# A 2 KB bias row fetched one unit ahead, and the first feed-forward weights used on the ready token blocks first

## The chip, the cores and the metric

One Trainium2 chip, 8 NeuronCores in two dies (cores 0 to 3, 4 to 7). The same program runs on all 8 cores, with no exchange between them. The metric is the device time of the slowest core in microseconds.

Engine names in profile lines: PE is TensorE (PEld its weight loads), DVE is VectorE, ACT is ScalarE, POOL is GpSimd, SP is SyncE; SPq marks the issue of a transfer by SP. In this kernel POOL issues the loads that cast from float32 to bf16 (all large weights), SP all other loads and all stores.

## The reference, cut to what matters

One layer of a diffusion backbone. Each core handles 12 tiles of 128 tokens (4 of context, 8 of latents). The order of the work on a core:

```
mod  = silu(c) @ w_ada + b_ada                 # six chunks of 2048; chunks 2 and 5 are the gates g1, g2
h    = modulate(rms_norm(x), sh1, sc1)
att  = differential_attention(h);  sgu = spatial_gating(h)
x1   = x + g1 * (concat(att, sgu) @ w_o)       # "projection"
h2   = modulate(rms_norm(x1), sh2, sc2)
y    = x1 + g2 * (relu(h2 @ w_ff1)**2 @ w_ff2) # "feed-forward", half of the time
```

The modulation matmuls are cut into 32 units. They run as filler between attention matmuls; units 16 to 31 make the gates, and each needs a row of 256 bias values for two conditions: 2 KB.

## The kernel before

The kernel has its own scheduler. It keeps an estimated clock for each engine and emits each instruction where that clock says TensorE would otherwise wait. So a change to one load changes the estimates, and with them the order of attention. In the traces every core runs the instructions of an engine in one and the same order, so an instruction that waits holds up those behind it. Cuts are marked `# ...`.

A gate unit. The bias row is loaded in the step that uses it:

```python
def ada_step():
    # ...
    ada_mm(wring[2], bank, 256)                  # 16 small matmuls
    mod_r.take()
    if chunk >= 2:
        S.load(brw, brow[chunk - 2, :, u * 256:(u + 1) * 256], "brw")
    nd = S.copy(modl, bank[:, 0:256])
    if i + 1 < 32:
        ada_dma1(i + 1)                          # 1 MB of weights for the next unit
    def fin(bj):
        # ...
            S.mm([(b2[0:2, 0:256], sel_t, modl, True, True)], 450)
            nd = S.tt(gst, b2[0:2, 0:256], brw, ALU.add)      # VectorE waits here for the bias
```

What is emitted after attention. POOL's queue runs ahead of TensorE, so these are issued as soon as their space is free:

```python
    for gi in range(4):
        wu_dma(gi)                               # gating "up" weights, 4 loads
    wo_dma(1)                                    # output projection, 1 of 4 blocks
    S.load(wsb, wsT, "wsb", cast=True)
    S.load(flat(bs_t), bsb, "bsb")
    S.load(sgw, sgunw, "sgw")                    # norm weights of the gating
```

The passage from the projection to the feed-forward. `norm2` normalises a finished token tile, and a delayed part `tr` transposes it on TensorE and, after every fourth tile, modulates 512 tokens on VectorE:

```python
    xm_r = Lot(S, [S.sbuf("xm%d" % i, [128, D], BF16, z1 + 8 * K + 4 * K * i) for i in range(2)])
    wf_r = [S.sbuf("wf%d" % i, [128, 4096], BF16, f0 + 8 * K * i) for i in range(2)]   # f0 = z1 + 8 K
    # ...
    for tt in range(12):
        wo_tile(tt)
        norm2(tt)
        wo_loads(tt + 3)
        if tt == 0:
            wf_dma()                             # first feed-forward weights
        S.pump()
    S.flush()                                    # the last tile's transposes and modulations
    wf_dma()                                     # second feed-forward weights
    # ...
    gate_load(1, g2_t)
    for tt in range(12):
        S.load(acc[:, tt, :], x1d[tt], "acc%d" % tt, dr=[("x1", tt)])     # residual
    for rd in range(8):
        for j in range(4):
            W = wf_s.pop(("1", rd, j)).rearrange("p (k n) -> p k n", k=16)
            for f in range(2):
                for tb in range(3):              # token blocks of 512
                    # 16 matmuls of 512 columns into one PSUM bank, relu (ACT), square (DVE)
            wf_dma()
        # then the four weight units of the second matrix
```

The first of the two feed-forward weight buffers lies over both `xm` buffers.

## Time and profile before

| | before |
|---|---|
| median of 3 runs | 2581.16 us |
| PE busy | 93% of the span |
| feed-forward, first to last matmul (core 2) | 1327.2 us, 6144 matmuls, 216 ns each |
| PE waits for an attention bank held up by the last bias load | 14.9 us (core 2) |
| PE waits for the last normalised tile | 5.5 us (all cores) |

The page of the slowest core (2) begins with the busy time of PE. Below it, in 40 slices of the span, stand the tenths in which PE was busy and its granted clock in tenths of full speed:

```profile
PE 2413.2 (93%) x16816; PEld 1390.6 (54%) x16816; DVE 1299.5 (50%) x2536; ACT 713.0 (28%) x1157; POOL 99.1 (4%) x164
...
PE   1469999999999979999999999999999999999999
...
PEclk9679999999999989999999999999999999999999
```

The reader sees an engine that is nearly always busy, with two visible weaknesses: the first tenth of the span, where the kernel waits for its first weights and which the change leaves alone, and one slice in the middle (the fifteenth, 904 to 968 us) with a lower digit in both rows. The last half of the rows is the feed-forward at full clock. There the change can win nothing.

**The slice in the middle.** POOL's queue at that time (columns: start, length, engine, line, operation, tiles; in brackets the idle time before it and what ended it). These weights are queued in two microseconds:

```profile
893.66 0.54 POOL L319 DMA_DIRECT2D wu_11985<-wu  x1
...
895.74 0.58 POOL L319 DMA_DIRECT2D wo_11994<-wo  x1
```

The same stretch on the other engines:

```profile
901.24 0.40 SPq L319 DMA_DIRECT2D brw<-brow  x1
...
905.91 0.59 PE L256 MATMUL ps<-modl,sel_t 128*2 128x256 f32 x2
...
909.89 1.02 ACT L272 ACTIVATE P_108<-ps 128x1024 bf16<-128x1024 f32 x1
923.20 0.41 DVE L288 TENSOR_TENSOR gst<-ps,brw 2x256 f32<-2x256 f32 x1 [17.43 <-DMA brw<-brow]
...
924.26 0.41 DVE L288 TENSOR_TENSOR o_115<-ps,st_67 128x256 f32<-128x256 f32 x1
...
924.82 1.02 PE L256 MATMUL ps<-VV_96,P_110 128*128 128x129 bf16 x8 [14.90 <-DVE o_115 L288]
```

The bias load is issued at 901.24. The unit's small matmul is done at 906.5. VectorE then sits until 923.20 for a 0.41 us addition, because the 2 KB have not landed. Behind it in VectorE's order is `o_115`, which empties an attention bank (a bank of PSUM, the memory that TensorE's results go to); TensorE has used up its other work by 909.9 us and waits for that bank. The view of waits for 895 to 925 us (total, times, longest) gives both:

```profile
DVE gst L288 <- DMA brw<-brow: 17.4, 1, 17.4
PE ps L256 <- DVE o_115 L288: 14.9, 1, 14.9
```

Two stores of attention results stand just ahead of the bias row in SP's own queue, at 899.8 and 900.8 us. The view of DMAs issued from 899.7 to 901.3 us (size, time from issue to landing) shows that they are late as well:

```profile
attd<-on_119 SPq DMA_DIRECT2D x1, 64.0 KB, 11.8
attd<-on_117 SPq DMA_DIRECT2D x1, 64.0 KB, 20.3
```

So the second store lands at 921.1 us. The single packets in the packed trace (`prof` has no view of them) say the same: the next two packets of 1 KB in that queue, which by size and order are the bias row, move only at 921.5 us. On all eight cores the store ahead of the row takes 20 to 26 us. By order and times the row waits behind slow stores in its own queue; what made that queue slow is tested below (weights_late).

**The start of the feed-forward.** The timeline from the last projection matmuls on:

```profile
1242.88 1.89 PE L256 MATMUL ps<-wo_11996,sguT 128*128 128x512 bf16 x8
...
1248.86 1.29 DVE L295 TENSOR_SCALAR xm_13138<-xw_13136,st_68 128x2048 bf16<-128x2048 f32 x1 [2.63 <-ACT st_68 L272]
...
1250.29 1.87 PE L263 MATMUL ps<-identb,xm_13138 128*128 128x128 bf16 x16 [5.52 <-DVE xm_13138 L295]
...
1251.95 4.28 PE L256 MATMUL ps<-hT,wf_13142 128*128 128x512 bf16 x13
1252.38 0.15 PEld L256 LDWEIGHTS ps<-hT,wf_13142 128*128 128x128 bf16 x1 [0.28 <-issue]
1252.40 3.97 DVE L295 TENSOR_SCALAR hT<-hT,A_47,S_48 128x512 bf16<-128x512 bf16 x12 [2.25 <-ACT hT L272]
1252.45 0.53 POOL L319 DMA_DIRECT2D wf_13141<-wf  x1 [179.37 <-PE ps L263]
1252.80 0.15 PEld L256 LDWEIGHTS ps<-hT,wf_13142 128*128 128x128 bf16 x1 [0.28 <-issue]
```

TensorE finishes the projection at about 1244.8, then waits 5.52 us while ACT and DVE normalise the last tile, and transposes it. The weight loads at 1252.38 and 1252.80 show the spacing of the first matmuls: 0.43 us and not 0.216. The modulations at 1252.40 are needed only by token block 2; blocks 0 and 1 were ready long before.

The Trainium skill, page "TensorE: Matmul & The Clock Gate", section "Part 1: The HAM clock gate", says that the array falls to half its clock after an idle window of about 3.4 us and comes back after about as long a busy one. The trace agrees: after both waits the granted clock reads 0.50, from 924.8 to 930.0 us and from 1250.0 to 1254.5 us.

### The profile page before, as it was taken

To read this page: it belongs to the slowest core of one execution; us is meant where nothing else is said; L and a number is where in the kernel's file an instruction comes from. 1 tells how busy PE (TensorE), PEld (TensorE's weight loads), DVE (VectorE), ACT (ScalarE), POOL (GpSimd) and SP (SyncE) were. 2 spreads that over 40 slices of the span, in tenths; PEclk is the share of its full clock that TensorE was granted. 3 is DMA by queue.
4 is the path that set the end of the run, shared out by engine and by line. 5 is a ranking of instruction groups with operands and counts; after the bars stand their busy time and mean duration, and the time that the engine had idled before them with its cause. 6 is when DMAs were issued, how large, how long until landed. Compare 5 with 4: busy or idle time off the path is not lost.

```text
span 2583.1 us, 39598 instructions; the slowest of 8 cores (2572.3 to 2583.1 us)
## 1 busy us (share of the span) xinstructions
PE 2413.2 (93%) x16816; PEld 1390.6 (54%) x16816; DVE 1299.5 (50%) x2536; ACT 713.0 (28%) x1157; POOL 99.1 (4%) x164
## 2 busy tenths in 40 slices
PE   1469999999999979999999999999999999999999
PEld 0358777777767765444444444444444444444444
DVE  1258563663663435455338165282562834717437
ACT  1146672773853753133210100101001010010110
POOL 0002100000000000000000000000000000000000
PEclk9679999999999989999999999999999999999999
DMA  9974543444355545744752332222222332222246
GB/s 188 189 191 129 83 89 68 85 81 80 66 92 103 97 86 87 175 166 144 186 140 50 55 57 52 49 49 50 49 49 52 57 56 49 49 49 49 50 94 184
DMA packets 58843, 237.17 MB, mean 92 GB/s; under 512 B 20336, under 2 KB 26032, under 8 KB 35376
## 3 DMA queue, kind: packets, MB, share of 16 engines
q0 software_dynamic: 22848, 150.25, 33.3%
q1 hardware_dynamic: 35824, 84.41, 10.0%
q8 instruction: 136, 2.23, 0.3%
q14 instruction: 35, 0.29, 0.0%
HBM read 352.34 MB, written 32.54 MB: 149 GB/s over the span
## 4 chain that ended last, share of the span: by engine, by line
PE 84%; DMA 8%; DVE 4%; ACT 3%; issue 0%; POOL 0%; another core or an unknown queue 0%; SPq 0%; DVEq 0%
PE ps L256 83%; DMA sel_t<-selsum 2%; DMA ada_122<-wa 2%; PE ps L263 1%; DMA xt_130<-xs 1%; DMA kr_106<-ck 1%; DMA wr_90<-wa 1%; DMA brw<-brow 1%; DMA kr_105<-ck 0%; DVE hT L295 0%; ACT P_110 L272 0%; ACT P_107 L272 0%; ACT P_109 L272 0%; DMA xt_129<-xs 0%
## 5 line engine op out<-in xcount | busy, mean ns | idle before, releaser
L256 PE MATMUL ps<-hT,wf_13142 128*128 128x512 bf16 x1536 | 335.4, 380 | 0.0
L256 PE MATMUL ps<-wf_13142,aT 128*128 128x512 bf16 x1536 | 334.1, 379 | 0.0
L256 PE MATMUL ps<-hT,wf_13141 128*128 128x512 bf16 x1536 | 334.1, 379 | 0.0
L256 PE MATMUL ps<-wf_13141,aT 128*128 128x512 bf16 x1536 | 334.1, 379 | 0.0
L272 ACT ACTIVATE rl_14431<-ps 128x512 f32<-128x512 f32 x96 | 57.3, 597 | 855.2 <-PE ps L256 855.2
L256 PEld LDWEIGHTS ps<-hT,wf_13142 128*128 128x128 bf16 x1536 | 150.4, 98 | 182.2 <-issue 1.7
L256 PEld LDWEIGHTS ps<-wf_13142,aT 128*128 128x128 bf16 x1536 | 150.5, 98 | 181.0
L256 PEld LDWEIGHTS ps<-hT,wf_13141 128*128 128x128 bf16 x1536 | 150.4, 98 | 181.1
L256 PEld LDWEIGHTS ps<-wf_13141,aT 128*128 128x128 bf16 x1536 | 150.2, 98 | 181.3
L288 DVE TENSOR_TENSOR aT<-rl_14432 128x512 bf16<-128x512 f32 x96 | 66.5, 693 | 264.9 <-ACT rl_14432 L272 264.9
L288 DVE TENSOR_TENSOR aT<-rl_14431 128x512 bf16<-128x512 f32 x96 | 66.5, 693 | 262.1 <-ACT rl_14431 L272 262.1
L288 DVE TENSOR_TENSOR tf_14433<-ps,g_t 128x512 f32<-128x512 f32 x192 | 132.8, 692 | 59.2 <-PE ps L256 59.2
L288 DVE TENSOR_TENSOR tf_14434<-ps,g_t 128x512 f32<-128x512 f32 x192 | 132.8, 692 | 58.8 <-PE ps L256 58.8
L256 PE MATMUL ps<-wr_88,hT 128*128 128x256 bf16 x1152 | 151.4, 284 | 6.9 <-DVE hT L295 4.6
L288 DVE TENSOR_TENSOR acc<-acc,tf_14434 128x512 f32<-128x512 f32 x192 | 132.9, 692 | 7.0
L288 DVE TENSOR_TENSOR acc<-acc,tf_14433 128x512 f32<-128x512 f32 x192 | 132.9, 692 | 7.0
L272 ACT ACTIVATE rl_14432<-ps 128x512 f32<-128x512 f32 x96 | 57.3, 597 | 274.2 <-PE ps L256 274.2
L256 PEld LDWEIGHTS ps<-wr_88,hT 128*128 128x128 bf16 x1152 | 111.7, 101 | 30.3 <-issue 15.5
L256 PE MATMUL ps<-wr_89,hT 128*128 128x256 bf16 x960 | 124.3, 276 | 0.7 <-ACT fz_97 L272 0.4
L272 ACT ACTIVATE P_107<-ps 128x1024 bf16<-128x1024 f32 x76 | 77.6, 1020 | 129.1 <-PE ps L256 129.1
L256 PEld LDWEIGHTS ps<-wr_89,hT 128*128 128x128 bf16 x960 | 91.0, 99 | 14.5 <-issue 4.1
L272 ACT ACTIVATE P_109<-ps 128x1024 bf16<-128x1024 f32 x76 | 77.5, 1019 | 30.8 <-PE ps L256 30.6
(802 smaller groups left out, 2827.7 us busy)
## 6 DMA issues: line engine op xcount, KB each, us to landing
wr_90<-wa POOLq DMA_DIRECT2D x32, 1024.0 KB, 9.2
wf_13142<-wf POOLq DMA_DIRECT2D x32, 1024.0 KB, 8.0
wf_13141<-wf POOLq DMA_DIRECT2D x32, 1024.0 KB, 8.0
acc<-x1d SPq DMA_DIRECT2D x12, 1024.0 KB, 42.1
ys<-acc SPq DMA_DIRECT2D x32, 256.0 KB, 2.4
ada_121<-wa POOLq DMA_DIRECT2D x3, 2048.0 KB, 26.5
ada_122<-wa POOLq DMA_DIRECT2D x3, 2048.0 KB, 38.9
wr_88<-wqkv POOLq DMA_DIRECT2D x6, 1024.0 KB, 10.1
```

What stands on the lines that cost most here:

```text
L256: ins = e.matmul(o, lhsT=l, rhs=r, start=st, stop=sp, skip_group_check=True)
L263: ins = e.transpose(o, i, ident)
L272: return self.add("act", lambda e: e.activation(out=out, in_=in_, func=func, bias=bias, scale=scale, **kw), reads=[in_] + aps, writes=[out ...
L288: return self.add(eng, lambda e: e.tensor_tensor(out=out, in0=a, in1=b, op=op), reads=[a, b], writes=[out], cost=self.dcost(eng, out, (a, b)))
```

## The change

Three intents. First, fetch the bias row one unit ahead, into a second buffer. Second, start the feed-forward with the token blocks that are ready, and put the last tile's transposes behind the first of that work; for this the second `xm` buffer moves away from under the weight buffer. Third, issue the second feed-forward weights earlier and mix the residual reloads between the weight loads.

```diff
-    brw = S.sbuf("brw", [2, 256], F32, p1 + 10 * K)
+    brw = [S.sbuf("brw%d" % i, [2, 256], F32, b) for i, b in enumerate((p1 + 10 * K, SB + 13 * K))]
@@ ada_step
-        if chunk >= 2:
-            S.load(brw, brow[chunk - 2, :, u * 256:(u + 1) * 256], "brw")
         nd = S.copy(modl, bank[:, 0:256])
         if i + 1 < 32:
+            c2, u2 = divmod(i + 1, 8)
+            if c2 >= 2:
+                S.load(brw[(i + 1) % 2], brow[c2 - 2, :, u2 * 256:(u2 + 1) * 256], "brw%d" % ((i + 1) % 2))
             ada_dma1(i + 1)
-                nd = S.tt(gst, b2[0:2, 0:256], brw, ALU.add)
+                nd = S.tt(gst, b2[0:2, 0:256], brw[i % 2], ALU.add)
@@ projection and feed-forward
-    xm_r = Lot(S, [S.sbuf("xm%d" % i, [128, D], BF16, z1 + 8 * K + 4 * K * i) for i in range(2)])
+    xm_r = [Lot(S, [S.sbuf("xm%d" % i, [128, D], BF16, b)]) for i, b in enumerate((z1 + 8 * K, SB + 10 * K))]
-    S.flush()
+    xm_r[0].take()
     wf_dma()
-    gate_load(1, g2_t)
-    for tt in range(12):
-        S.load(acc[:, tt, :], x1d[tt], "acc%d" % tt, dr=[("x1", tt)])
     for rd in range(8):
         for j in range(4):
-            for f in range(2):
-                for tb in range(3):
+            late = rd == 0 and j == 0
+            for f, tb in [(f, tb) for tb in range(3) for f in range(2)] if late else [...]:
+                    if late and (f, tb) == (0, 2):
+                        S.flush()
+                        gate_load(1, g2_t)
                     ...
+                        S.pump()
             wf_dma()
+            if rd == 0:
+                for tt in range(3 * j, 3 * j + 3):
+                    S.load(acc[:, tt, :], x1d[tt], "acc%d" % tt, dr=[("x1", tt)])
```

More of the change, by code (lines that the diff above doesn't have):

```diff
@@ L1307, in norm2 @@
         xw = xw_s.pop(tt)
-        xm = xm_r.take()
+        xm = xm_r[tt % 2].take()
         S.store(x1d[tt], xw, "x1d%d" % (tt % 3), dw=[("x1", tt)])
@@ L1314, in tr @@
             norm_c(xm, lambda k0, n: h2T[:, k0:k0 + n, tt * 128:(tt + 1) * 128], b8, ("act", "act"))
-            xm_r.give(xm)
+            xm_r[tt % 2].give(xm)
             if tt % 4 == 3:
@@ L1362, in build_program @@
             W = wf_s.pop(("1", rd, j)).rearrange("p (k n) -> p k n", k=16)
-            for f in range(2):
-                for tb in range(3):
+            late = rd == 0 and j == 0
+            for f, tb in [(f, tb) for tb in range(3) for f in range(2)] if late else [(f, tb) for f in range(2) for tb in range(3)]:
+                    if late and (f, tb) == (0, 2):
+                        S.flush()
+                        gate_load(1, g2_t)
                     zj = b8.take()
```

## The prediction

> **What bounds it now.** TensorE. The page's first part gives PE 2413.2 of 2583.1 us (93%); the chain of waits is 83% matmuls. From 1252.2 us to the end the chain is one unbroken run of 6144 feed-forward matmuls, 216 ns each, at clock 1.00: nothing is to be won there. The change can only win in two stalls of PE that the timeline shows, on every core:
>
> 1. *Bias stall, 909.9 to 924.8 us (core 2).* The last 2 KB bias-row load is issued at 901.2 us, after the up- and output-projection weights were queued at 893 to 896 us, and takes 21.9 us. VectorE, in order, waits 17.4 us for it; the attention normalisation behind it holds the PSUM bank, and PE waits 14.9 us ("PE <- DVE o"). Over the cores: 15.0 to 15.6 us (0, 2, 4, 7), 18.6 to 19.1 us (1, 3, 5, 6). Afterwards matmuls run at half speed until about 929.7 us (129-column groups 1.02 us, not 0.62): some 2.5 us more.
> 2. *Start of feed-forward, 1244.8 to 1252.2 us.* PE waits 5.5 us (all cores) for the normalised last token tile, transposes it (1.87 us, not 1.06 as for earlier tiles), and its first six matmuls are 0.43 us apart. The first weight unit takes 22.0 us, the next 20.7: 1.3 us lost.
>
> The Trainium skill, "TensorE: Matmul & The Clock Gate", Part 1, says that an idle window of about 3.4 us drops the array to half clock; both stalls agree.
>
> **What the change does.** The last bias load moves one unit ahead, to about 888 us, before the weights are queued: the other 15 loads show at most 2.5 us of waits in total. Stall 1 goes.
> The first feed-forward unit takes token blocks 0 and 1 first. The instruction order shows the last tile's transposes after 32 feed-forward matmuls, 6.9 us after the projection ends; the tile is ready 5.4 us after it, so slack is 1.5 us. The 16 modulations (5.3 us on VectorE) then have 6.9 us of matmuls to hide behind. Stall 2 goes, perhaps with half a microsecond left where block 2 starts.
> The second feed-forward weights are issued some 12 us earlier: worth nothing, they landed in 16.4 us and had 21.5. The residual reloads move only in program order: SyncE's order there is unchanged and their waits end at the same moment. The third weight load, issued about 1266 us amid them, must land within 20.7 us; its kind took 15.4.
>
> The scheduler also reshuffles attention between about 590 and 905 us (one modulation unit earlier, small swaps). PE is 93% busy there, its waits many and under 3.1 us: I expect noise of a few microseconds either way.
>
> **Sum, cores 2 and 4 (the slowest):** 14.9 + 2.5 + 5.5 + 0.8 + 1.3 = 25 us. Cores 1, 3, 5, 6 gain 29 but are not the slowest. 2581.2 - 25 = **2556 us**, 8 in 10: **2549 to 2565**. Chances: faster by over 2% 0.02, within 2% 0.96, slower by over 2% 0.02.
>
> **What would show it.** No wait of VectorE on the bias load over 3 us after 850 us; no "PE <- DVE o" near 15 us; no PE wait on the last normalised tile; first feed-forward unit 20.7 us plus 1.1 us of transposes; feed-forward still 1327 us; clock between 780 and 950 us up from 0.95 towards 0.99.
>
> **What would make it wrong.** The new attention order adds or removes PE waits; the gating's weight, bias and norm loads, now nearer the output weights in flight, hold VectorE or PE; the modulations finish late for block 2; the third weight load exceeds 20.7 us.

## More of the kernel before

In some executions one die, sometimes both, runs at a visibly lower granted TensorE clock and takes up to 18% longer, whatever the kernel. Such runs are called slow here and are left out.

## The result, and the profile after

| | before | after |
|---|---|---|
| median of 4 runs, slow ones included | 2581.28 us | 2554.07 us |
| fast runs | 2580.1, 2581.2, 2581.4 | 2553.3, 2553.7, 2554.5 |
| ratio of fast runs | | 0.9895, interval 0.9873 to 0.9918 |

A ratio is the mean time of one kernel's fast runs over that of the other's fast runs of the same rounds, so it is not quite the ratio of the medians. The slow runs are one before (2949.3 us) and two after (2889.1 and 2981.3 us, the last not in the median). The change takes off 27 us; 25 were predicted, and the measured time lies within the stated range.

The page after (slowest core 6), the same three rows:

```profile
PE 2408.7 (94%) x16816; PEld 1387.7 (54%) x16816; DVE 1298.9 (51%) x2536; ACT 712.4 (28%) x1157; POOL 99.0 (4%) x164
...
PE   1469999999999999999999999999999999999999
...
PEclk9679999999999999999999999999999999999999
```

The low slice in the middle is gone from both rows. Between 780 and 950 us the granted clock of the slowest core is 1.00, where it was 0.95 before.

The answer to the bias stall, from 894 to 922 us:

```profile
895.99 0.32 SPq L319 DMA_DIRECT2D brw_114<-brow  x1
...
899.92 0.54 POOL L319 DMA_DIRECT2D wu_11988<-wu  x1
...
901.99 0.58 POOL L319 DMA_DIRECT2D wo_11997<-wo  x1
...
913.11 0.41 DVE L308 COPY modl<-ps 128x256 f32<-128x256 f32 x1
...
915.00 0.59 PE L256 MATMUL ps<-modl,sel_t 128*2 128x256 f32 x2
...
917.19 0.41 DVE L288 TENSOR_TENSOR gst<-ps,brw_114 2x256 f32<-2x256 f32 x1
```

The last bias row is now issued at 895.99, before the weights queued from 899.92 on, and is used at 917.19, 21 us later. The addition follows with no idle time noted before it. The waits of PE from 870 to 960 us, complete:

```profile
PE ps L256 <- ACT P_108 L272: 0.7, 1, 0.7
PE ps L256 <- issue: 0.4, 1, 0.4
PE ps L256 <- DVE o_116 L288: 0.3, 1, 0.3
PE ps L256 <- ACT P_110 L272: 0.2, 1, 0.2
```

The start of the feed-forward:

```profile
1216.26 0.53 POOL L319 DMA_DIRECT2D wf_13143<-wf  x1 [165.07 <-PE ps L263]
...
1220.98 1.89 PE L256 MATMUL ps<-wo_11999,sguT 128*128 128x512 bf16 x8
...
1222.70 7.07 PE L256 MATMUL ps<-hT,wf_13144 128*128 128x512 bf16 x32
...
1229.61 1.06 PE L263 MATMUL ps<-identb,xm_13140 128*128 128x128 bf16 x16
...
1230.50 13.98 PE L256 MATMUL ps<-hT,wf_13144 128*128 128x512 bf16 x64
...
1231.32 5.26 DVE L295 TENSOR_SCALAR hT<-hT,A_47,S_48 128x512 bf16<-128x512 bf16 x16 [2.47 <-ACT hT L272]
...
1244.32 1.89 PE L256 MATMUL ps<-hT,wf_13143 128*128 128x512 bf16 x8
```

TensorE goes from the projection's last group (1220.98) into the feed-forward (1222.70) with no wait, runs 32 matmuls, transposes the tile in 1.06 us, and goes on. (The delayed part comes this early because of the new `S.pump()` calls; the `S.flush()` before token block 2 is only its latest place.) The modulations (1231.32 to 1236.58) hide behind the next 32 matmuls. The first weight unit takes 1244.32 - 1222.70 = 21.6 us, transposes included; 20.7 + 1.1 had been predicted. The second weights are issued at 1216.26.

One wait is new. VectorE's waits from 870 to 960 us contain

```profile
DVE gn L288 <- DMA sgw<-sgunw: 8.4, 1, 8.4
```

for the gating's norm weights, which are now fetched while the output weights are in flight: they land 13.4 us after their issue, and took 4.9 us before. PE's own list above shows nothing that follows from it.

**Where the time went, by stage.** From the times of the first and last instruction of each stage. In every undisturbed run one core of each neighbouring pair (0/1, 2/3, 4/5, 6/7) is slower, and which one changes from run to run. The metric follows the slower ones, so the table gives the mean over the slower core of each pair, and in brackets over the faster ones, in us:

| stage | before | after | difference |
|---|---|---|---|
| to the first attention softmax | 271.9 (270.3) | 271.4 (270.1) | -0.5 (-0.2) |
| to the first gate unit | 349.7 (347.1) | 350.7 (346.8) | +1.0 (-0.3) |
| to the last attention matmul | 313.8 (313.6) | 291.5 (286.9) | -22.3 (-26.7) |
| to the first "up" matmul of the gating | 42.6 (42.6) | 44.0 (44.1) | +1.4 (+1.5) |
| to the last projection matmul | 263.6 (263.6) | 263.6 (263.5) | 0.0 (-0.1) |
| to the first feed-forward matmul | 7.6 (7.6) | 0.2 (0.2) | -7.4 (-7.4) |
| feed-forward | 1326.9 (1326.6) | 1326.8 (1326.8) | -0.1 (+0.2) |

The sum is -27.8 (-32.8). The feed-forward start fits to a tenth. The gate stage gives 5 us more than the stall that was counted there, and 1.4 us come back in the gating stage.

### The profile page after: what moved, and what is told of

The parts are those of the page before. It is cut to its first block, busy times and chain, and to the rows that moved or that the text cites. A ratio compares the mean times of both kernels' runs of the same rounds, so it can differ in the third digit from the quotient of the medians.

```text
span 2553.4 us, 39598 instructions; the slowest of 8 cores (2541.4 to 2553.4 us)
## 1 busy us (share of the span) xinstructions
PE 2408.7 (94%) x16816; PEld 1387.7 (54%) x16816; DVE 1298.9 (51%) x2536; ACT 712.4 (28%) x1157; POOL 99.0 (4%) x164
## 4 chain that ended last, share of the span: by engine, by line
PE 87%; DMA 6%; DVE 3%; ACT 2%; issue 0%; another core or an unknown queue 0%; POOL 0%; SPq 0%; DVEq 0%
PE ps L256 85%; DMA sel_t<-selsum 2%; DMA ada_123<-wa 1%; PE ps L263 1%; DMA xt_131<-xs 1%; DMA kr_106<-ck 1%; DVE hT L295 0%; DMA kr_105<-ck 0%; ACT P_108 L272 0%; ACT P_107 L272 0%; DMA xt_130<-xs 0%; ACT P_110 L272 0%; ACT P_109 L272 0%; DVE xn_127 L295 0%
```

## The experiments

Eleven kernels ran, in three calls, each call on another chip and with its own runs of the kernel before. All gave correct results. On all three chips many runs were slow, and some that count as fast had a die at clock 0.963 to 0.973 and lasted some 10 to 30 us longer. Of the kernel before in the second call five of eight fast runs were such, so the ratios of the calls are blurred. I therefore compare runs in which all eight cores had a clock of at least 0.975, a limit chosen with the results in view, and give their mean:

| call | kernel | runs | mean, us | against |
|---|---|---|---|---|
| 1 | before | 5 | 2582.2 | |
| 1 | bias_only | 4 | 2561.8 | -20.5 |
| 1 | ff_only | 3 | 2575.4 | -6.8 |
| 1 | bias_old_order | 5 | 2565.3 | -16.9 |
| 1 | weights_late | 4 | 2567.4 | -14.8 |
| 2 | before | 3 | 2585.4 | |
| 2 | reload_front (same instruction order as after) | 5 | 2554.8 | -30.6 |
| 2 | plain_order | 5 | 2560.6 | +5.8 to reload_front |
| 2 | second_late (same program as after) | 2 | 2557.0 | +2.2 to reload_front |
| 2 | ck_later | 4 | 2550.6 | -4.2 to reload_front |

The ratios of fast runs as computed, with the disturbed ones in them, are 0.9941, 0.9974, 0.9934 and 0.9943 for the first call in that order, 0.9835, 0.9851, 0.9855 and 0.9814 for the second, and 0.9885, 0.9884 and 0.9882 for the third (after_again, second_shared, sgw_early). In the third call die 1 ended 8 us or more behind die 0 in every fast run, so there I compare the slower core of die 0 alone: before 2580.6 (5 runs), after_again 2551.6 (4), second_shared 2554.8 (3), sgw_early 2552.5 (4).

My theory after the result: (a) the bias stall is 15 us of waiting and 2.5 us of half clock; (b) the feed-forward start is 7.5 us; (c) the other 3 to 4 us come from the new attention order, which nobody aimed at. Rivals: the feed-forward part is worth more than (b); or the bias load is late for another reason than the weights in flight.

### bias_only: the bias part alone

The diff is the first two hunks of the change.

> The gate bias part of the change alone. My theory (the stall of the last bias load is 14.9 us of TensorE waiting and 2.5 us of half clock after it, and the new attention order is worth about 3 to 4.5 us more, as the changed kernel's trace suggests): 20 to 22 us off the kernel before. Rival (the gain of the changed kernel is the stall alone and the rest came from the feed-forward part): 17 us off.

Measured: -20.5 us. The wait for the last bias row is gone, the 5.5 us before the feed-forward are still there. This agrees with the theory and not with 17.

### ff_only: the feed-forward part alone

The diff is the rest of the change.

> The feed-forward part alone, bias load as before. My theory: 7 to 8 us off (5.5 us of waiting for the last normalised tile, 0.8 us of slow transposes, 1.3 us of slow first matmuls), and the bias stall of about 15 us still in the trace. Rival (the feed-forward part is worth more, because earlier second weights and interleaved reloads matter as well): 10 us or more off.

Measured: -6.8 us, a little under the 7 to 8 expected. In its trace the gap before the feed-forward falls from 7.6 to 0.2 us on all cores, and the bias stall stands as before (waits from 890 to 925 us):

```profile
DVE gst L288 <- DMA brw<-brow: 16.5, 1, 16.5
...
PE ps L256 <- DVE o L288: 14.0, 1, 14.0
```

The rival of 10 us or more falls. And -20.5 - 6.8 = -27.3: the parts add up to the whole.

### bias_old_order: the early bias with the order of before

To tell the stall from the new order. The real load is moved ahead; the scheduler's estimates are fed with what the old load would have done:

```diff
+    def early_bias(i):
+        keep = S.et["sp"], S.dma_t
+        bias_nd[i] = S.load(brw[i % 2], ..., "brw%d" % (i % 2))
+        S.et["sp"], S.dma_t = keep
+    def old_clock(i):                       # where the load stood before: only its estimate
+        t0 = S.et["sp"]
+        if i - 1 in gst_nd:
+            t0 = max(t0, gst_nd[i - 1].t + 130, bias_nd[i - 1].t + 130)
+        S.et["sp"] = t0 + 60
+        S.dma_t = max(S.dma_t, t0 + 60) + 2048 / DMA_RATE
+        bias_nd[i].t = S.dma_t + 2000
```

The instruction order of PE, DVE, ACT and POOL came out identical to before; only SP's differs.

> The bias rows are fetched one unit ahead, but the scheduler's clock is kept as it was, so that every engine but the load queue has exactly the instruction order of the kernel before. If the stall alone is worth 14.9 + 2.5 us on the slower cores: 17 to 18 us off. If the new attention order of the changed kernel is worth nothing, this equals bias_only; my theory says bias_only is faster than this by 3 to 4 us.

Measured: -16.9 us. PE's waits from 880 to 960 us, complete:

```profile
PE ps L256 <- DMA wr<-wa: 1.4, 1, 1.4
PE ps L256 <- DVE o L288: 0.2, 1, 0.2
PE ps L256 <- ACT P L272: 0.2, 1, 0.2
```

In the trace that is kept, the stage from the first gate unit to the last attention matmul is 17.5 us shorter than before on the slower cores (20.2 on the faster ones): the waits of 15 (19) us and some 2 to 3 us of half clock. That is term (a), within a microsecond. The distance to bias_only, 3.5 us, is the attention order, as the theory said. In the traces the gaps between matmuls from the first softmax to the first "up" matmul, counting those of 0.3 us or more, sum to 20 to 27 us over the cores in bias_old_order and to 17 to 23 us in bias_only: the new order has fewer of them. It is luck of the scheduler: bias_old_order has the early bias and not this gain.

### weights_late: nothing fetched earlier, the weights issued later

```diff
+    S.load(wsb, wsT, "wsb", cast=True)      # waits for the end of attention
     for gi in range(4):
         wu_dma(gi)
     wo_dma(1)
-    S.load(wsb, wsT, "wsb", cast=True)
```

> The kernel before with one line moved: the small mixing-matrix load, which waits for the end of attention, goes ahead of the up- and output-projection weights in their queue, so that these are issued after the last bias load and not 7 us before it. Nothing is fetched earlier. If the weights in flight are the cause of the 21.9 us bias load, the load takes 2 to 4 us, the stall goes, and 14 to 18 us come off. Rival (the load is late because it is issued only one step before its use, whatever is in flight): the stall stays and the time is within 2 us of before.

Measured: -14.8 us. The bias is loaded where it was, and the stall is gone: PE waits at most 0.2 us for an attention bank from 880 to 960 us. The instruction order of every engine but POOL is that of the kernel before. So the bias row was late because of the weights queued ahead of it, and the rival falls. The store ahead of it in SP's queue, which took 20 to 26 us before, now lands in 1.7 to 2.5 us on all cores: the weights slowed that queue. Whether the row would have been quick under the same weights without the two stores ahead of it, or on another queue, was not tested. The remaining 2 us against bias_old_order are partly seen: the weights now compete later, VectorE waits 11 to 14 us for the norm weights, and from the first "up" matmul to the last projection matmul the kept trace is 1.4 us longer than before on the slower cores.

### reload_front: the residual reloads back in front

```diff
+    for tt in range(12):
+        S.load(acc[:, tt, :], x1d[tt], "acc%d" % tt, dr=[("x1", tt)])
     for rd in range(8):
@@
-            if rd == 0:
-                for tt in range(3 * j, 3 * j + 3):
-                    S.load(acc[:, tt, :], x1d[tt], "acc%d" % tt, dr=[("x1", tt)])
```

> The changed kernel with the twelve residual reloads back in front of the feed-forward loop. Every engine's instruction order and waits come out identical to the changed kernel's, so this is also the control of this call: 26 to 28 us off the kernel before, first feed-forward unit 21.6 us as in the changed kernel. A rival that says the interleaving helps expects it 2 us or more slower than that.

Measured: -30.6 us, more than the 26 to 28 expected, on a chip where the kernel before (3 runs) was 3 us slower than in the first call. The order of all engines is the same as in the changed kernel, so the interleaving is empty: SP has nothing else to do there and issues the reloads when their space is free, wherever they stand in the source. What the run tells is the spread: the same change was worth 27 to 31 us.

### second_late: an experiment that tested nothing

```diff
-    xm_r[0].take()
-    wf_dma()
@@ in the loop, where (f, tb) == (0, 2)
                         S.flush()
+                        wf_dma()
                         gate_load(1, g2_t)
```

> The changed kernel, but the second feed-forward weights are issued only after the last tile's transposes, as in the kernel before. My prediction said issuing them earlier is worth nothing: then 0 against reload_front. Rival, which I now hold for likelier: the first unit no longer waits for the transposes, so a load issued 8.2 us into it and landing 16.4 us later comes at 24.6 us, 3 us after the first unit's end at 21.6: 3 to 4.5 us slower than reload_front, with TensorE waiting for wf by DMA in the trace.

Measured: 2557.0 against 2554.8 us, from two undisturbed runs. The reading is void: the program is instruction for instruction that of the changed kernel. POOL runs ahead of TensorE, so moving the statement moves nothing. What lets the load go early is the new place of the second `xm` buffer. The 2.2 us are thus a measure of the noise of few runs; one of the two has cores at a clock of 0.976 and 0.977, where no core of reload_front's five runs is below 0.979.

### second_shared: the same question, mended

```diff
-    xm_r = [... enumerate((z1 + 8 * K, SB + 10 * K))]
+    xm_r = [... enumerate((z1 + 8 * K, z1 + 12 * K))]
```

on top of second_late. Now the weights lie over the last tile again and must wait for its transposes.

> The mended second_late, which had come out as the very same program as the changed kernel. Here the two normalised-tile buffers lie where they lay before, so the second feed-forward weights, which share their space, really cannot be issued before the last tile's transposes. My prediction (issuing them earlier is worth nothing): 0 against after_again. Rival, which I hold for likelier: issued 8.2 us into the first unit and landing 16.4 us later, 3 us after the first unit's end at 21.6: 3 to 4.5 us slower, with TensorE waiting for wf by DMA.

Measured, on the slower core of die 0: 2554.8 against 2551.6 us, +3.2. On core 0 the timeline shows the load and the first matmul that uses it:

```profile
1227.50 0.53 POOL L319 DMA_DIRECT2D wf<-wf  x1 [179.79 <-PE ps L263]
...
1244.08 6.27 PE L256 MATMUL ps<-hT,wf 128*128 128x512 bf16 x21 [3.06 <-DMA wf<-wf]
```

The waits are 3.1, 0.7, 1.8 and 2.4 us on cores 0 to 3. The prediction's "worth nothing" falls, as the rival said. On core 0 the feed-forward is 4.8 us longer, more than the wait. The windows show why (columns: stretch, its length, busy time of PE, PEld, DVE, ACT, POOL with counts; then clock, DMA share and GB/s):

```profile
1241.00:1244.00 3.00, 0.01 (x1) 0.00 (x0) 0.69 (x1) 0.60 (x1) 0.53 (x1) 0.98 0.80 178
1244.00:1247.00 3.00, 2.92 (x7) 1.05 (x8) 0.00 (x0) 0.00 (x0) 0.00 (x0) 0.50 1.03 229
```

The clock is halved after the gap of 3.1 us.

### plain_order: the block order of before in the first unit

```diff
-            for f, tb in [(f, tb) for tb in range(3) for f in range(2)] if late else [...]:
+            for f, tb in [(f, tb) for f in range(2) for tb in range(3)]:
```

> The changed kernel, but the first weight unit keeps the old order of token blocks (0, 1, 2 for one half of the weights, then for the other), so that block 2 comes right after the last tile's transposes. Theory: the 16 modulations of 0.33 us each on VectorE are then on the path, the third group waits 3.5 us for the first eight of them and the next 1 us: 4 to 6 us slower than reload_front. Rival (moving the transposes behind two groups is enough, the swapped order does nothing): within 1 us of reload_front.

Measured: +5.8 us. The transposes stand behind 32 matmuls as in the changed kernel, but the next group needs block 2 (slowest core 4):

```profile
1230.01 1.06 PE L263 MATMUL ps<-identb,xm 128*128 128x128 bf16 x16
...
1231.71 5.26 DVE L295 TENSOR_SCALAR hT<-hT,A,S 128x512 bf16<-128x512 bf16 x16 [2.48 <-ACT hT L272]
...
1234.91 27.32 PE L256 MATMUL ps<-hT,wf 128*128 128x512 bf16 x117 [3.85 <-DVE hT L295]
1234.91 0.15 PEld L256 LDWEIGHTS ps<-hT,wf 128*128 128x128 bf16 x1 [0.28 <-issue]
```

TensorE waits 3.5 to 4.4 us on all cores for the modulations, and on core 4 the granted clock reads 0.50 afterwards. The feed-forward takes 1331.2 to 1332.1 us and not 1326.8. So the transposes' place is not enough; the swapped order is worth about as much as the wait that the change removes.

### sgw_early: is the new wait of VectorE a cost?

```diff
-    sgw = S.sbuf("sgw", [128, 1024], F32, p1 + 6 * K)
+    sgw = S.sbuf("sgw", [128, 1024], F32, SB + 6 * K)     # free after the last K and Q tables
@@ in filler_g, at the first step with no open K, Q chain
+                    S.load(sgw, sgunw, "sgw")              # estimates kept as they were
```

> The changed kernel with the gating norm weights loaded about 100 us earlier into space that attention has left, every other instruction order as in the changed kernel. It takes away the 8 us that VectorE now waits for them amid the output weights. Theory (TensorE has enough queued and free banks, the wait is off the path): within 1.5 us of after_again. Rival (the new wait gives back part of the gain): 2 us or more faster.

Measured, slower core of die 0: 2552.5 against 2551.6 us, no gain. On core 0 VectorE no longer waits for it. The stage to the first "up" matmul is 44.0 us on die 0 with and without. So the 8 us are off the path; the 1.4 us by which that stage grew against before are matmuls moved behind attention by the new order, not a wait.

after_again was the control of this call:

> Control: the changed kernel itself, 26 to 31 us off the kernel before, with VectorE waiting about 8 us for the gating norm weights (sgw) and TensorE waiting for nothing there.

Measured: -29.0 us on die 0.

### ck_later: an attempt at a better version

```diff
-        S.after(nd, lambda: with_bank(lambda j: to_cols(kr, KT[s], 2560, p, j)), 500)
+        S.after(nd, lambda: with_bank(lambda j: to_cols(kr, KT[s], 2560, p, j)), 6000 if p else 500)
```

The waits of the changed kernel's slowest core for the cached keys, from 270 to 650 us, are

```profile
PE ps L263 <- DMA kr_106<-ck: 2.6, 2, 1.6
...
PE ps L263 <- DMA kr_105<-ck: 1.1, 1, 1.1
```

and only one core of each pair has them.

> An attempt at a better version: the changed kernel with the scheduler told that the cached keys of head pairs 1 to 3 arrive 5.5 us later than it thinks, so that TensorE turns to their transposes later. In the changed kernel the slower core of each pair waits 1.1 + 2.6 us for these loads. If only that goes: 2 to 4 us faster than reload_front. The scheduler reorders attention from there on, which has been worth 4 us in one direction already, so a loss of up to 5 us is possible.

Measured: 2550.6 us, 4.2 less than the changed kernel of the same call, and the fastest of all. In its trace no core's list for that stretch has a wait for the cached keys in it. The two cores of a pair are now 2.5 to 3.6 us apart in the profiled run, where they were 9.0 to 10.6 apart in the changed kernel's. How much of the 4.2 us is these waits and how much another order of attention is not separated.

## Why the prediction was right

- **Bias stall, 17.4 us.** Right, shown twice: bias_old_order (-16.9; 17.5 in its stage) and weights_late. Its cause, the weights queued ahead, is shown by weights_late. The prediction did not see that two late stores stood ahead of the row in SP's queue.
- **Start of the feed-forward, 7.6 us.** Right: -7.4 in the stages, -6.8 in ff_only. The transposes came after 32 matmuls with no wait, and the half microsecond allowed for block 2 was not needed.
- **No gain from interleaved reloads.** Right: the instruction order and waits are identical.
- **New attention order: "noise of a few microseconds either way".** This term was set to zero and came out at -3.5 us (bias_only against bias_old_order). It is the mis-sized term of the sum, and with a little spread of the others it is what separates 27 from 25. The prediction gave no sign to it, and I found nothing in the trace of before that would have. The other two terms came to 16.9 + 6.8 = 23.7 us, so the total would have stayed in the range without it; that the new order helped and did not hurt was luck.
- **"Second weights earlier: worth nothing, they landed in 16.4 us and had 21.5."** This step was wrong. The 21.5 us were counted on the old timeline, where the first unit stood behind the transposes. When the unit starts 7.4 us earlier, the same load comes up to 3.1 us too late. Without the early issue the change would have lost 3.2 us of its gain. It did not move the total, since the changed kernel has the early issue.
- **Gating loads might hold VectorE or PE.** They hold VectorE 8.4 us and PE not at all (sgw_early).

## What to carry to other kernels

Look for waits on tiny loads that were issued just after large ones, and at what stands ahead of them in their own queue: a 2 KB row behind two 64 KB stores cost 17 us here, and either fetching it earlier or issuing the large loads later removed it. When a phase starts with work that is not ready, reorder the first unit so that ready data comes first, then recompute the slack of everything that the old wait used to hide: the second weights had slack only thanks to the stall. Before an experiment on the place of a statement is run, compare the instruction orders; a queue that runs ahead makes many source moves empty.

## What the Trainium skill lacked or had wrong

- "TensorE: Matmul & The Clock Gate", section "Part 1: The HAM clock gate", gives about 3.4 us of idle time for the drop to half clock. Here shorter gaps were followed by a granted clock of 0.50, all in second_shared: one of 3.06 us (core 0, 1244 to 1247 us), one of 2.9 us (core 0, 407.7 to 414.4 us) and one of 2.5 us (core 1, 756.9 to 760.0 us). After one of 2.4 us (core 3, 1243.4 to 1246.0 us) it stayed at 1.00. The 3.4 us should not be read as a safe limit. The same page's closing table has about 3 us, which is nearer and not safe here either.
- "DMA: Bandwidth & Descriptors", section "Anatomy of one DMA", fits a transfer issued from GpSimd with about 2 us of fixed cost plus its bytes, and says nothing of what is in flight beside it. In this kernel a 2 KB load issued from SyncE took about 22 us (901.24 to 923.20) with weights in flight on the other queue and two stores ahead of it in its own. The same page, section "Queues, rings and completion order", says that a completion update lands only after all earlier writes of that DMA engine, across its queues. That is not the main part here: the packets of the row themselves move only at 921.5 us, 20.2 us after the issue (before, core 2). The fit would do well to warn of what is already queued.
- No page that I read says that neighbouring cores differ: in the three fast runs of the result one core of each pair takes 2551 to 2553 us and the other 2541 to 2544 (for instance 2552.0 and 2541.4 on cores 0 and 1), with the roles changing from run to run. In the profiled run the waits for the cached keys are on the slower ones alone. Why one of the pair gets its loads later is open.
- No page has the intermediate state: a die at a mean clock of 0.963 to 0.973, some 10 to 30 us longer, between the fast and the slow runs.
